# A gated three-branch token mixer: another first head, and weight sums made by the DMA

## The chip, the cores and the metric

The kernel runs on one core of one Trainium2 chip. The metric is the device time of one execution in microseconds (us); the median of the runs is what is compared.

## The reference

One layer over 512 tokens of width 2048, one batch, all in float32. The input is normed and projected once; the columns of this projection are the queries, keys, values and gate paths of three branches with four heads of 128 each, one forget logit per head, and three merge gates of width 2048.

```python
def hybrid_layer(x, norm_g, w_in, b_f, b_gate, qk_norm_g, rel_bias, w_up, w_out):
    hn = rmsnorm(x, norm_g)                       # x * rsqrt(mean(x*x) + 1e-6) * g
    proj = jnp.einsum('bsd,dc->bsc', hn, w_in)    # 2048 -> 3*4*512 + 4 + 3*2048 columns
    br = proj[..., :QKVG_COLS].reshape(b, s, N_BRANCH, 4, BRANCH_W)
    f_logit = proj[..., QKVG_COLS:QKVG_COLS + N_HEADS] + b_f
    gates = jax.nn.sigmoid(proj[..., QKVG_COLS + N_HEADS:] + b_gate).reshape(b, s, N_BRANCH, D_MODEL)
    ...                                           # A: forgetting attention, B: chunked attention with a
    ...                                           # relative bias, C: stick-breaking attention
    ys = jnp.stack([ya, yb, yc], axis=2) * jax.nn.silu(br[:, :, :, 3])
    up = jnp.einsum('bsnw,nwd->bsnd', ys, w_up)
    merged = jnp.sum(gates * up, axis=2)
    return x + jnp.einsum('bsd,de->bse', merged, w_out)
```

## The kernel before, in words

x lies transposed in 16 tiles of 128 rows of the model dimension by 512 tokens. TensorE's rounded float32 type is used throughout: every operand is split into a high part (ACT, L92) and a low part (DVE, L93), and `mm3` (L101 to L103) sums three products: high with high, low with high, high with low.

Most columns are computed two column tiles at a time. `pair_task` multiplies the 2x2 blocks of two tiles' weights (a11, a12 of the one, a21, a22 of the other, by halves of the model dimension) with the 2x2 blocks of x (halves of the model dimension by halves of the tokens) in seven products in place of eight, in Winograd's form of Strassen's method. One product is 8 k tiles of 3 matmuls of 256 columns. x's sides of products 1, 2, 3 and 5 are x's own parts (`x1`, `x2`) and a sum T1, those of 6, 7 and 4 are the sums T2, T3 and T4, made once by `combos`. The weights' sides of products 5, 7, 6 and 3 are sums of raw weight tiles: before, a pair loads its four raw tiles (512 KB each, `raw`, six buffers) through SP's queue, and DVE makes four sums of 128x1024 (L315 and those behind it). The order of the products is 1, 2, 6, 7, 4, 5, 3.

The program is a list of units (a product of a pair, or half a column by itself). The loop at the end runs through it: weights are split two units ahead of their matmuls (`prep_to`, `wh` and `wl`, three buffers each) and loaded seven units ahead (`load_to`). Its order for PE is kept as written for the first units (`OFF["man"]`); elsewhere a scheduler sets each engine's order.

`first_head` starts the run. Its units are the two halves of the forget logits (32 matmuls of 512 columns, x's high and low parts in turn) between those of Q and K, then V and G of the first head, each column by itself: 16 k tiles of 3 matmuls of 512 columns. `prep_x` splits x times its gain before the norm is known, and squares x; POOL and DVE share the running sum of squares. `norm_x` sums over the partitions with two full-precision matmuls (L247), and `rsqrt` makes rstd on ACT and DVE (L235 to L240), which is multiplied into Q, K, V, G as they leave PSUM. Then `combos` scales x itself (L255, DVE) and makes T2, T3 and T4 (L257 to L260, POOL), and `parts1`, `parts2` split the scaled x a second time into the same tiles. Two pairs of merge gate columns follow, then the other heads.

In all there are 54 pairs: 24 of gates, 22 of the heads (Q with K, V with G) and 8 of the output projection; the up projections are 32 units of 18 matmuls of 512 columns.

Of the kernel before, what the change touches and what calls it, by code (L numbers as in the profile page):

```python
# [38 lines left out]
def hybrid_kernel(  # L39
# [60 lines left out]
    def mm3(ps, lh, ll, rh, rl, start, stop):  # L100
        nc.tensor.matmul(ps, lh, rh, start=start, stop=False)  # L101
        nc.tensor.matmul(ps, lh, rl, start=False, stop=False)  # L102
        nc.tensor.matmul(ps, ll, rh, start=False, stop=stop)  # L103

    # ------------------------------------------------------------------ constants
# [18 lines left out]
    class Unit:  # L124
        """A stretch of the tensor engine's work with one stationary operand of up to 8 k tiles."""

        def __init__(self, shape, prep, mms, srcs=(), after=None):
            self.shape, self.prep, self.mms, self.srcs, self.after = shape, prep, mms, srcs, after
            self.hi = self.lo = None
# [4 lines left out]
    def load(u):  # L134
        u.raw = []
        for s, keep in u.srcs:
            t = raw_tile(u.shape)
            nc.sync.dma_start(t, s)
            u.raw.append(t)
            if keep is not None:  # L140
                keep.append(t)

    def prep(u):
        if u.shape is None:
            return
        u.hi = wp.tile([P] + u.shape, F32R, tag="wh", name=nm("wh"), bufs=LA + 1)
        u.lo = wp.tile([P] + u.shape, F32R, tag="wl", name=nm("wl"), bufs=LA + 1)
        u.prep(u)

    def prep_raw(u):  # L150
        split_to(u.hi, u.lo, u.raw[0])

    for kt in range(4):
        load_x(kt)
# [18 lines left out]
    # -1 where key k >= j: suffix sums inside a block  # L173
# [4 lines left out]
    # A, rows are queries: NEG where the key (free) is after the query  # L178
# [4 lines left out]
    # C, rows are keys: valid where the query (free) is after the key  # L183
# [7 lines left out]
    # column h has ones on the rows h, 32 + h, 64 + h, 96 + h  # L191
# [6 lines left out]
    # the query gains carry the softmax scale  # L198
# [16 lines left out]
    sqp = [att(), att()]  # L215

    def prep_x(kt):
        x = xraw[kt]
        h, lo = xs[kt]
        if kt % 2:  # L220
            nc.vector.tensor_scalar_mul(h, x, gn[:, kt:kt + 1])
        else:
            nc.scalar.activation(h, x, AF.Copy, scale=gn[:, kt:kt + 1])
        nc.vector.scalar_tensor_tensor(lo, x, gn[:, kt:kt + 1], f(h), op0=ALU.mult, op1=ALU.subtract)
        s = sqp[kt // 2 % 2] if kt % 2 and kt > 1 else t2("sq")
        nc.scalar.activation(s, x, AF.Square)
# [23 lines left out]

    def combos(k):
        """The rows of x at their norm, and what Strassen's form needs of them beside the parts."""
        a, b = xraw[k], xraw[k + UK]
        for x, kt in ((a, k), (b, k + UK)):
            nc.vector.scalar_tensor_tensor(x, x, gn[:, kt:kt + 1], rstd[0], op0=ALU.mult, op1=ALU.mult)  # L255
        t, u = t2("t23"), t2("t4")
        nc.gpsimd.tensor_sub(t[:, RH], b[:, RH], a[:, RH])  # L257
        nc.gpsimd.tensor_sub(a[:, RH], a[:, RH], a[:, LH])
        nc.gpsimd.tensor_sub(t[:, LH], b[:, RH], a[:, RH])
        nc.gpsimd.tensor_sub(u[:, LH], t[:, LH], b[:, LH])  # L260
        split_to(*t23[k], t)
        split_to(t4[k][:, LH], t4[k][:, RH], u[:, LH])
# [8 lines left out]
    # ------------------------------------------------------------------ projections  # L271
# [12 lines left out]
    def col_task(srcs, xs, evac):  # L284
        """A column tile as it stands; two units, one for each half of the rows."""
        ps = Lazy(acc)

        def mms(i):
            def go(u):
                for j in range(UK):  # L290
# [4 lines left out]
                     srcs=[(srcs[i], None)],  # L295
                     after=(lambda: evac(ps())) if i == 1 else None) for i in range(2)]

    def pair_task(src1, src2, ops, done, late=False, before_last=None):
        """Two column tiles by seven products in place of eight (Strassen, in Winograd's form).

        late: the products with T2, T3 and T4 come last."""
        kept = []
        st = {}
        w = {}
        order = (1, 2, 5, 3, 6, 7, 4) if late else (1, 2, 6, 7, 4, 5, 3)

        def prep_of(i):
            p = order[i]

            def go(u):  # L310
                if i == 0:
                    w[1], a21, w[4], w[2] = kept
                    split_to(u.hi, u.lo, w[1])
                    w[5] = raw_tile()
                    nc.vector.tensor_add(w[5], a21, w[4])  # L315
                    if late:
                        nc.vector.tensor_sub(a21, w[1], a21)
                        nc.vector.tensor_sub(w[1], w[5], w[1])
                    w[7], w[6], w[3] = a21, w[1], w[2]
                    return  # L320
                split_to(u.hi, u.lo, w[p])
                if i == 1:
                    if not late:
                        nc.vector.tensor_sub(w[7], w[1], w[7])
                        nc.vector.tensor_sub(w[6], w[5], w[1])
# [4 lines left out]
        def mms_of(i):  # L330
            def go(u):
                st["ps"] = ps = acc()[:, LH]
                for j in range(UK):
                    mm3(ps, u.hi[:, j, :], u.lo[:, j, :], *ops[order[i]](j), j == 0, j == UK - 1)
            return go

        def after_of(i):
            p = order[i]

            def go():  # L340
                ps = st["ps"]
# [8 lines left out]
                elif p == 6:  # L350
                    add(u[:, LH], u[:, LH], ps)
                    if late:
                        add(c1[:, RH], c1[:, RH], u[:, LH])
                elif p == 7:
                    add(u[:, RH], u[:, LH], ps)
                    if late:
                        add(c2[:, RH], c2[:, RH], u[:, RH])
# [4 lines left out]
                elif p == 5:  # L362
                    add(c2[:, RH], u[:, RH], ps)
                    add(u[:, LH], u[:, LH], ps)
                elif late:
                    add(c1[:, RH], c2[:, RH], ps)
                else:
                    add(c1[:, RH], u[:, LH], ps)
# [6 lines left out]
        src = {0: [(src1[0], kept), (src2[0], kept), (src2[1], kept), (src1[1], kept)]}  # L375
# [535 lines left out]
```

## Time and profile before

| what | us |
|---|---|
| median of 3 runs | 1400.05 (1399.22 to 1400.08) |
| span of the profiled execution | 1397.6 |
| PE busy | 1366.3 (98%) |
| DVE busy | 1191.8 (85%) |
| ACT busy | 729.7 (52%) |
| POOL busy | 53.7 (4%) |

The span is that of the instructions of one profiled execution; the median of the runs lies 2.45 us above it. PE is matmuls, DVE is VectorE, ACT is ScalarE, POOL is GpSimd, SP issues most of the DMAs. A row of a group of instructions reads: line, engine, operation, output<-input, shape and type, count, then busy time in all, mean time of one in ns, and the idle time before them with what ended it. A row of the chain of waits reads: start, duration, engine, what, line, count. Of a table of stages: the stretch and its length, busy time and count for PE, PEld (weight loads), DVE, ACT and POOL, then the granted clock of TensorE, the busy share of the DMA engines, and GB/s.

### The profile page before, as it was taken

The numbers are of one execution on the slowest core, as the hardware profiler recorded it, in microseconds if no ns is written. First come the engines' busy times: TensorE is split into PE (matmuls) and PEld (weight loads), VectorE is DVE, ScalarE is ACT, GpSimd is POOL, SyncE is SP. The second block draws the span as 40 slices with busy tenths as digits, with TensorE's granted clock in tenths as the row PEclk, the third lists the DMA queues.
The fourth block names the chain that finished last, engine by engine and source line by source line (L and its number), as shares of the span: only waits on it lengthen the run. The fifth ranks groups of instructions, "written<-read, shape, count | busy, mean of one in ns | idle before, by whom it ended". The sixth has DMA issues, their size and how long they took to land.

```text
span 1397.6 us, 25474 instructions
## 1 busy us (share of the span) xinstructions
PE 1366.3 (98%) x10452; PEld 1316.7 (94%) x10452; DVE 1191.8 (85%) x1671; ACT 729.7 (52%) x1042; POOL 53.7 (4%) x60
## 2 busy tenths in 40 slices
PE   6969999999999999999999999999999999999999
PEld 3759999999999999999999999999999988899999
DVE  8999898887978889888888888888888888898886
ACT  6345564544545555555556555545555755453332
POOL 4730000000000000000000000000000000000000
PEclk9989999999999999999999999999999999999999
DMA  7113334323344244342433333333233766535542
GB/s 272 46 46 106 122 102 126 121 91 114 106 129 126 95 114 128 113 129 95 117 122 115 121 94 119 113 114 121 91 115 103 273 197 203 169 109 176 164 151 76
DMA packets 63093, 176.39 MB, mean 126 GB/s; under 512 B 7400, under 2 KB 9320, under 8 KB 62976
## 3 DMA queue, kind: packets, MB, share of 16 engines
q1 hardware_dynamic: 59520, 170.49, 38.4%
q10 hardware_dynamic: 3456, 4.26, 0.8%
q8 instruction: 82, 1.34, 0.4%
q14 instruction: 35, 0.29, 0.1%
HBM read 155.04 MB, written 19.69 MB: 125 GB/s over the span
## 4 chain that ended last, share of the span: by engine, by line
PE 92%; DVE 5%; issue 1%; ACT 0%; POOL 0%; DMA 0%; SPq 0%; DVEq 0%; ACTq 0%; POOLq 0%
PE acc L101 27%; PE acc L103 27%; PE acc L102 27%; PE att L103 3%; PE att L101 3%; PE att L102 3%; DVE x L255 1%; DVE wl L93 1%; PE att L548 1%; PE att L517 1%; PE att L570 1%; DVE x1l L93 1%; PE att L571 1%; PE att L569 1%; DVE t23l L93 0%
## 5 line engine op out<-in xcount | busy, mean ns | idle before, releaser
L92 ACT ACTIVATE wh<-raw 128x1024 fp32r<-128x1024 f32 (+1 forms) x418 | 435.7, 1043 | 549.2 <-PE acc L102 488.2
L93 DVE TENSOR_TENSOR wl<-raw,wh 128x1024 fp32r<-128x1024 f32 (+1 forms) x418 | 503.9, 1206 | 96.7 <-ACT wh L92 95.9
L102 PE MATMUL acc<-x1l,wh 128*128 128x256 f32 (+1 forms) x768 | 222.3, 289 | 10.5 <-DVE x1l L93 10.5
L103 PE MATMUL acc<-x1h,wl 128*128 128x256 f32 (+1 forms) x768 | 222.0, 289 | 2.2 <-DVE wl L93 2.2
L101 PE MATMUL acc<-x1h,wh 128*128 128x256 f32 (+1 forms) x768 | 223.7, 291 | 0.0
L101 PE MATMUL acc<-x2h,wh 128*128 128x256 f32 (+1 forms) x768 | 223.6, 291 | 0.0
L102 PE MATMUL acc<-x2l,wh 128*128 128x256 f32 (+1 forms) x768 | 221.9, 289 | 0.9 <-DVE x2l L93 0.9
L103 PE MATMUL acc<-x2h,wl 128*128 128x256 f32 (+1 forms) x768 | 221.8, 289 | 0.0
L101 PE MATMUL acc<-t23h,wh 128*128 128x256 f32 x736 | 209.7, 285 | 0.0
L103 PE MATMUL acc<-t23h,wl 128*128 128x256 f32 x736 | 208.4, 284 | 0.0
L102 PE MATMUL acc<-t23l,wh 128*128 128x256 f32 x736 | 208.1, 283 | 0.0
L102 PEld LDWEIGHTS acc<-x1l,wh 128*128 128x128 f32 x768 | 147.8, 192 | 13.4 <-DVE x1l L93 11.2
L103 PEld LDWEIGHTS acc<-x1h,wl 128*128 128x128 f32 x768 | 147.8, 193 | 3.9 <-DVE wl L93 2.4
L102 PEld LDWEIGHTS acc<-x2l,wh 128*128 128x128 f32 x768 | 148.0, 193 | 2.4 <-DVE x2l L93 1.1
L101 PEld LDWEIGHTS acc<-x1h,wh 128*128 128x128 f32 x768 | 147.9, 193 | 1.8 <-issue 0.2
L101 PEld LDWEIGHTS acc<-x2h,wh 128*128 128x128 f32 x768 | 148.2, 193 | 1.3
L103 PEld LDWEIGHTS acc<-x2h,wl 128*128 128x128 f32 x768 | 148.0, 193 | 1.3
L101 PEld LDWEIGHTS acc<-t23h,wh 128*128 128x128 f32 x736 | 141.0, 192 | 0.5
L102 PEld LDWEIGHTS acc<-t23l,wh 128*128 128x128 f32 x736 | 141.0, 192 | 0.1
L103 PEld LDWEIGHTS acc<-t23h,wl 128*128 128x128 f32 x736 | 140.7, 191 | 0.3
L101 PE MATMUL acc<-t,wh 128*128 128x256 f32 x368 | 105.1, 286 | 0.0
L102 PE MATMUL acc<-t,wh 128*128 128x256 f32 x368 | 104.4, 284 | 0.0
(256 smaller groups left out, 2728.0 us busy)
## 6 DMA issues: line engine op xcount, KB each, us to landing
raw<-in_w_col SPq DMA_DIRECT2D x192, 512.0 KB, 3.6
raw<-in_w_out SPq DMA_DIRECT2D x32, 512.0 KB, 3.8
gl<-c SPq DMA_DIRECT2D x48, 256.0 KB, 2.0
raw<-in_w_up SPq DMA_DIRECT2D x32, 384.0 KB, 3.2
sg<-gl SPq DMA_DIRECT2D x48, 256.0 KB, 5.0
x<-in_xT SPq DMA_DIRECT2D x16, 256.0 KB, 5.4
xr<-in_xT SPq DMA_DIRECT2D x16, 256.0 KB, 4.4
yd<-y SPq DMA_DIRECT2D x11, 256.0 KB, 2.0
```

What stands on the lines that cost most here:

```text
L92: nc.scalar.activation(hi, src, AF.Copy)
L93: nc.vector.tensor_sub(lo, src, f(hi))
L101: nc.tensor.matmul(ps, lh, rh, start=start, stop=False)
L102: nc.tensor.matmul(ps, lh, rl, start=False, stop=False)
L103: nc.tensor.matmul(ps, ll, rh, start=False, stop=stop)
L255: nc.vector.scalar_tensor_tensor(x, x, gn[:, kt:kt + 1], rstd[0], op0=ALU.mult, op1=ALU.mult)
L517: nc.tensor.transpose(ps[:, blk(i)], st["p"][i][:, blk(j)], identf)
L548: nc.tensor.matmul(ps[:, i * P:], nu_r if i == j else nones_r, part, start=i == j and part is st["lk"][j][0], stop=False)
L569: nc.tensor.matmul(o, vh[:, blk(j)], st["h"][j], start=j == 0, stop=False)
L570: nc.tensor.matmul(o, vl[:, blk(j)], st["h"][j], start=False, stop=False)
L571: nc.tensor.matmul(o, vh[:, blk(j)], st["l"][j], start=False, stop=j == QB - 1)
```

## The change

*The first head.* x is scaled by its gain in place and is not split before the norm. Q and K (`first_pair`) are plain full-precision products of the raw weights with the scaled x, 2 x 16 matmuls of 512 columns; their weights are not split, and their raw halves are loaded between the x tiles, with quarters at first. ACT makes all squares, and DVE alone sums them. The sum over the partitions stands behind k tile 9 of Q and K. `split_x` then multiplies rstd into x and splits it, once; V and G and the forget logits use these parts and leave PSUM by a plain copy on ACT. `combos` works in place on x's halves, all on DVE, with T2 and T4 of the other sign, and `split_t1`, `split_t` split halves of 128x256. The order of the units is Q and K, V, G, V, G, the two halves of the forget logits, and then two gate pairs whose seven products alternate (1 of one, 1 of the other, 2, 2 and so on).

*The pairs.* With the signs changed every weight sum is an addition. Product 5's and product 7's weights are loaded as one raw tile by SP, onto which an accumulating DMA from POOL's queue (L324 of the changed kernel) adds the second; DVE makes the two that are left from them (6 is 5 plus 1, 3 is 6 plus 2, in place). The order is 5, 1, 2, 6, 7, 4, 3, and product 3 goes on in product 5's PSUM bank. In the two interleaved gate pairs and the first output pair ("late": 1, 2, 3, 5, 6, 7, 4) products 6 and 3 are made by accumulating DMAs too, two and three of them in a chain on one buffer. An ordinary pair moves 7 raw tiles in place of 4 (two for 5 and for 7, one each for 1, 2 and 4), a late one 14 (three for 6 and four for 3 besides).

```diff
-    def mm3(ps, lh, ll, rh, rl, start, stop):
+    def mm3(ps, lh, ll, rh, rl, start, stop, more=False):
...
     def load(u):
-        u.raw = []
-        for s, keep in u.srcs:
-            t = raw_tile(u.shape)
-            nc.sync.dma_start(t, s)
-            u.raw.append(t)
...
+        if u.load is not None:
+            u.load(u)
+        elif u.src is not None:
+            u.raw = raw_tile(u.shape)
+            nc.sync.dma_start(u.raw, u.src)
...
     def prep_x(kt):
         x = xraw[kt]
-        h, lo = xs[kt]
-        if kt % 2:
-            nc.vector.tensor_scalar_mul(h, x, gn[:, kt:kt + 1])
-        else:
-            nc.scalar.activation(h, x, AF.Copy, scale=gn[:, kt:kt + 1])
-        nc.vector.scalar_tensor_tensor(lo, x, gn[:, kt:kt + 1], f(h), op0=ALU.mult, op1=ALU.subtract)
-        s = sqp[kt // 2 % 2] if kt % 2 and kt > 1 else t2("sq")
+        s = t2("sq")
         nc.scalar.activation(s, x, AF.Square)
+        nc.scalar.activation(x, x, AF.Copy, scale=gn[:, kt:kt + 1])
         if kt < 2:
             ssq[kt] = s
         else:
-            (nc.gpsimd, nc.vector)[kt % 2].tensor_add(ssq[kt % 2], ssq[kt % 2], s)
+            nc.vector.tensor_add(ssq[kt % 2], ssq[kt % 2], s)
...
+    def split_x(kt):
+        nc.vector.tensor_mul(xraw[kt], xraw[kt], rstd[0])
+        split_to(*xs[kt], xraw[kt])
+
     def combos(k):
         a, b = xraw[k], xraw[k + UK]
...
+        nc.vector.tensor_sub(a[:, LH], a[:, LH], a[:, RH])
+        nc.vector.tensor_sub(a[:, RH], b[:, RH], a[:, RH])
+        nc.vector.tensor_add(b[:, RH], b[:, RH], a[:, LH])
+        nc.vector.tensor_sub(b[:, LH], b[:, RH], b[:, LH])
+
+    def split_t1(k):
+        (h, lo), a = x1[k], xraw[k]
+        split_to(h[:, RH], lo[:, RH], a[:, LH])
+
+    def split_t(k):
+        (h, lo), a, b = t23[k], xraw[k], xraw[k + UK]
+        split_to(h[:, LH], lo[:, LH], b[:, RH])
+        split_to(h[:, RH], lo[:, RH], a[:, RH])
+        split_to(t4[k][:, LH], t4[k][:, RH], b[:, LH])
...
-        order = (1, 2, 5, 3, 6, 7, 4) if late else (1, 2, 6, 7, 4, 5, 3)
+        order = (1, 2, 3, 5, 6, 7, 4) if late else (5, 1, 2, 6, 7, 4, 3)
+        (a11, a12), (a21, a22) = src1, src2
+        parts = {1: [a11], 2: [a12], 4: [a22], 5: [a21, a22], 7: [a11, a21]}
+        if late:
+            parts.update({6: [a21, a22, a11], 3: [a21, a22, a11, a12]})
+
+        def load_of(i):
+            def go(u):
+                p = order[i]
...
+                w[p] = raw_tile()
+                nc.sync.dma_start(w[p], parts[p][0])
+                for src in parts[p][1:]:
+                    nc.gpsimd.dma_start(w[p], src, accum_op=ALU.add)
+            return go
...
             def go(u):
-                if i == 0:
-                    w[1], a21, w[4], w[2] = kept
-                    split_to(u.hi, u.lo, w[1])
-                    w[5] = raw_tile()
-                    nc.vector.tensor_add(w[5], a21, w[4])
...
                 split_to(u.hi, u.lo, w[p])
-                if i == 1:
-                    if not late:
-                        nc.vector.tensor_sub(w[7], w[1], w[7])
-                        nc.vector.tensor_sub(w[6], w[5], w[1])
-                if i == (1 if late else 4):
-                    nc.vector.tensor_sub(w[3], w[3], w[6])
+                if not late and p == 1:
+                    w[6] = w[5]
+                    nc.vector.tensor_add(w[6], w[6], w[1])
+                elif not late and p == 6:
+                    w[3] = w[6]
+                    nc.vector.tensor_add(w[3], w[3], w[2])
...
+                more = p == 3 and not late
+                st[p] = ps = st[5] if more else acc()[:, LH]
...
+    def first_pair(st, n, h):
...
+            load_x(0)
+            w(Q, 0, 0, h4)
+            w(K, 0, 0, h4)
+            for kt in range(1, UK):
+                load_x(kt)
+            w(Q, 0, h4, UK)
+            w(K, 0, h4, UK)
+            for kt in range(UK, KT):
+                load_x(kt)
+            for r in cols:
+                w(r, 1, 0, UK)
+
+        def mms(u):
+            for kt in range(KT):
+                for r in cols:
+                    nc.tensor.matmul(ps[r](), raw[r, kt // UK][:, kt % UK, :], xraw[kt],
+                                     start=kt == 0, stop=kt == KT - 1)
+                if kt == OFF["ssq"]:
+                    with tc.high_priority():
+                        norm_x()
+
+        def after():
+            for kt in range(KT):
+                split_x(kt)
+            for r in cols:
+                st[r] = t2("c")
+                nc.vector.tensor_mul(st[r], ps[r](), rstd[0])
...
-        units.extend([fu[0], c[Q][0], c[K][0], fu[1], c[Q][1], c[K][1],
-                      c[V][0], c[G][0], c[V][1], c[G][1]])
+        units.extend([first_pair(st, n, h), c[V][0], c[G][0], c[V][1], c[G][1], fu[0], fu[1]])
+        pairs = []
+        for _ in range(2):
+            u0 = len(units)
+            gate_units(late=True)
+            pairs.append(units[u0:])
+            del units[u0:]
+        units.extend(u for two in zip(*pairs) for u in two)
...
-    prep_to(1)
-    load_to(2)
...
+    load_to(1)
+    for kt in range(KT):
+        prep_x(kt)
+    load_to(4)
...
-OFF = dict(cs=4, ct=12, nk=5, nq=4, s=12, t=16, v=1, av=8, a0=11, b0=18, c0=3, c1=2, man=17, last=3, l1=0, l2=0)
+OFF = dict(tf=2, cs=4, ct=12, nk=5, nq=4, s=12, t=16, v=1, av=8, ssq=9, fb=10, a0=8, b0=15, man=14, last=3)
```

The order of ACT's instructions before rstd. Before, ACT squares x (`sq`, `att`), scales some of it (`x2h`), splits weights (`wh`), and starts rstd (L235):

```order
L226 ACTIVATE att_194<-x_223 128x512
L92 ACTIVATE wh_372<-raw_310 128x1024
L226 ACTIVATE sq_301<-x_225 128x512
L226 ACTIVATE att_195<-x_227 128x512
L223 ACTIVATE x2h_185<-x_221,small_in 128x512
L92 ACTIVATE wh_403<-raw_312 128x1024
L223 ACTIVATE x2h_189<-x_225,small_in 128x512
L235 ACTIVATE rt_363<-att_359,epsc 128x512
```

In the changed kernel (`wh_303`, `wh_307` and `wh_412` are V's first half, G's first half and V's second half; rstd starts at L226):

```order
L92 ACTIVATE wh_307<-raw_297 128x1024
L216 ACTIVATE sq_279<-x_221 128x512
L217 ACTIVATE x_219<-x_219,small_in 128x512
L216 ACTIVATE sq_283<-x_223 128x512
L217 ACTIVATE x_221<-x_221,small_in 128x512
L217 ACTIVATE x_223<-x_223,small_in 128x512
L92 ACTIVATE wh_412<-raw_299 128x1024
L216 ACTIVATE sq_287<-x_225 128x512
L216 ACTIVATE sq_291<-x_227 128x512
L217 ACTIVATE x_225<-x_225,small_in 128x512
L217 ACTIVATE x_227<-x_227,small_in 128x512
L226 ACTIVATE rt_339<-att_335,epsc 128x512
```

The last two squares now stand behind three weight splits, all of V and G.

DVE's instructions up to the last low part of x's first half in the changed kernel, where L244 is the multiplication by rstd, L93 the low part and L670 the evacuation of Q:

```order
L244 TENSOR_TENSOR x_223<-x_223,rstd_338 128x512
L93 TENSOR_TENSOR x1l_144<-x_201,x1h_143 128x512
L93 TENSOR_TENSOR x1l_146<-x_203,x1h_145 128x512
L244 TENSOR_TENSOR x_225<-x_225,rstd_338 128x512
L93 TENSOR_TENSOR x1l_148<-x_205,x1h_147 128x512
L670 TENSOR_TENSOR c_408<-acc_313,rstd_338 128x512
L93 TENSOR_TENSOR x1l_150<-x_207,x1h_149 128x512
L244 TENSOR_TENSOR x_227<-x_227,rstd_338 128x512
L93 TENSOR_TENSOR x1l_152<-x_209,x1h_151 128x512
```

All 16 multiplications by rstd stand ahead of the last low part of x1; before, the 16 operations of L255 stood there one behind the other, with x's parts already in use by Q and K.

POOL's queue behind its constants, in the changed kernel (`raw_566` is product 3 of the first gate pair, `raw_607` that of the second; 635 and 719 are their products 5, 763 and 806 their products 6, 862 and 895 their products 7):

```order
L324 DMA raw_566<-in_w_col 128x1024 x3
L324 DMA raw_607<-in_w_col 128x1024 x2
L324 DMA raw_635<-in_w_col 128x1024
L324 DMA raw_607<-in_w_col 128x1024
L324 DMA raw_719<-in_w_col 128x1024
L324 DMA raw_763<-in_w_col 128x1024 x2
L324 DMA raw_806<-in_w_col 128x1024
L324 DMA raw_862<-in_w_col 128x1024
L324 DMA raw_806<-in_w_col 128x1024
```

Where the sums of squares and T2 to T4 stood on POOL, only these DMAs stand now, in this order in one queue.

More of the change, by code (lines that the diff above doesn't have):

```diff
@@ L150, in prep_raw @@
     def prep_raw(u):
-        split_to(u.hi, u.lo, u.raw[0])
-    for kt in range(4):
-        load_x(kt)
+        split_to(u.hi, u.lo, u.raw)
     epsc = cp.tile([P, 1], F32, name="epsc")
@@ L340, in go @@
             def go():
[L341 removed]
+                ps = st[p]
                 if i == 0:
@@ L361, in go @@
                     nc.scalar.activation(c2[:, RH], ps, AF.Copy)
[L362 to L368, printed above, removed]
+                    add(c1[:, RH], c1[:, RH], ps)
+                elif p == 3 and late:
+                    nc.scalar.activation(c1[:, RH], ps, AF.Copy)
+                elif p == 3:
+                    sub(c1[:, RH], ps, u[:, LH])
                 if i == 5 and before_last is not None:
@@ L373, in after_of @@
             return go
-        src = {0: [(src1[0], kept), (src2[0], kept), (src2[1], kept), (src1[1], kept)]}
-        return [Unit([UK, P], prep_of(i), mms_of(i), srcs=src.get(i, ()), after=after_of(i)) for i in range(7)]
+        return [Unit([UK, P], prep_of(i), mms_of(i), load=load_of(i), after=after_of(i)) for i in range(7)]
     side = {}
@@ L621, in hybrid_kernel, with load, w, kept @@
     cur = [0]
-    def scaled(st, r):
+    def first_pair(st, n, h):
+        cols = {r: col(n, r, h) for r in (Q, K)}
+        raw = {}
+        ps = {r: Lazy(acc) for r in cols}
+        def load(u):
+            def w(r, i, a, b):
+                if (r, i) not in raw:
+                    raw[r, i] = raw_tile()
+                nc.sync.dma_start(raw[r, i][:, a:b, :], cols[r][i][:, a:b, :])
+            h4 = UK // 2
+            load_x(0)
[23 more added lines that the diff above has]
+                nc.vector.tensor_mul(st[r], ps[r](), rstd[0])
+        return Unit(None, None, mms, load=load, after=after)
+    def kept(st, r):
         def evac(ps):
             st[r] = t2("c")
-            nc.vector.tensor_mul(st[r], ps, rstd[0])
+            nc.scalar.activation(st[r], ps, AF.Copy)
         return evac
@@ L631, in first_head, with sums, forget @@
         fu, fps = f_units()
[L632 to L641 removed]
+        c = {r: col_task(col(n, r, h), xs, kept(st, r)) for r in (V, G)}
+        units.extend([first_pair(st, n, h), c[V][0], c[G][0], c[V][1], c[G][1], fu[0], fu[1]])
[6 more added lines that the diff above has]
+        units.extend(u for two in zip(*pairs) for u in two)
+        def sums():
+            for k in range(UK):
+                combos(k)
         def parts1():
             for k in range(UK):
[L645 removed]
+                split_t1(k)
         def parts2():
             for k in range(UK):
[L649 removed]
+                split_t(k)
+        def forget():
             v = t2("f")[:2 * NH, :]
[L651 removed]
+            nc.scalar.activation(v, fps[:2 * NH, :], AF.Copy)
             nc.sync.dma_start(fd, v)
[L653 to L655 removed]
+            at(OFF["fb"], forget_bias)
+        at(OFF["tf"], sums)
+        at(5, parts1)
+        at(6, forget)
+        at(7, parts2)
         a, b = head_stages(n, h, st)
[L657 to L658 removed]
         for d, g in a:
```

85 lines of the change are left out of this document (21 added, 64 removed).

## The prediction

> **What bounds the kernel now.** I read the profile's page first: the engines' shares, the forty slices and the chain that ended last.
>
> ```profile
> span 1397.6 us, 25474 instructions
> PE 1366.3 (98%) x10452; PEld 1316.7 (94%) x10452; DVE 1191.8 (85%) x1671; ACT 729.7 (52%) x1042; POOL 53.7 (4%) x60
> ...
> PE   6969999999999999999999999999999999999999
> ...
> POOL 4730000000000000000000000000000000000000
> ...
> PE 92%; DVE 5%; issue 1%; ACT 0%; POOL 0%; DMA 0%; SPq 0%; DVEq 0%; ACTq 0%; POOLq 0%
> ```
>
> TensorE (PE) is the bound; 31 us of the span are not PE's, nearly all in the first three slices, where POOL has its only work. So I cut the run into stages (us, then busy time and instruction count by engine, granted clock, DMA share, GB/s).
>
> ```profile
> 0.00:95.00 95.00, 68.98 (x274) 49.50 (x274) 88.59 (x113) 46.29 (x74) 52.18 (x57) 0.93 0.33 118
> 95.00:1235.00 1140.00, 1139.98 (x8877) 1110.88 (x8878) 970.50 (x1383) 619.69 (x893) 1.51 (x3) 1.00 0.40 125
> 1235.00:1262.00 27.00, 24.98 (x202) 24.17 (x201) 25.77 (x40) 15.34 (x26) 0.00 (x0) 1.00 0.36 117
> 1262.00:1394.00 132.00, 132.00 (x1103) 132.00 (x1102) 106.52 (x137) 48.33 (x50) 0.00 (x0) 1.00 0.45 145
> ```
>
> From 95 us on PE has no idle time but 2.0 us between 1235 and 1262. In 0 to 95 us PE ran 274 instructions: 192 of the four columns Q, K, V, G, 32 of the forget logits, 4 of the sum of squares, which leaves 46 of the first pair of columns. The chain of waits names what holds PE there, VectorE (DVE):
>
> ```profile
> 6.02 0.60 ACT att L226
> 6.63 0.65 ACT x1h L223
> ...
> 33.82 0.70 DVE rw L239
> 34.61 0.70 DVE rstd L240
> ...
> 37.33 9.25 DVE x L255 x8
> ...
> 88.09 0.60 DVE x1l L93
> 88.69 0.61 DVE x2l L93
> ...
> 92.89 0.33 DVE t L93
> 93.23 1.14 DVE wl L93
> 94.36 0.61 DVE x2l L93
> ...
> 95.02 0.39 PE acc L102
> 95.41 0.12 PE acc L103
> 95.52 0.12 PE acc L101
> ```
>
> A matmul of 256 columns takes 0.12 us in a row of them. Had PE done nothing of the pairs before and run them without a gap, they would have begun at 95.0 - 46 x 0.12 = **89.5 us**. Everything behind is PE end to end, so the change is worth what it does to that moment, plus what it frees or adds at PE later.
>
> **The pace of single pieces**, from the order of time:
>
> ```profile
> 9.50 2.17 ACT L226 ACTIVATE sq<-x 128x512 f32<-128x512 f32 x4
> ...
> 20.55 0.63 PE L101 MATMUL acc<-x1h,wh 128*128 128x512 f32 x1
> 20.97 0.63 PE L102 MATMUL acc<-x1l,wh 128*128 128x512 f32 x1
> ...
> 25.64 0.40 PE L101 MATMUL acc<-x1h,wh 128*128 128x512 f32 x1
> 25.87 0.39 PE L102 MATMUL acc<-x1l,wh 128*128 128x512 f32 x1
> ...
> 28.37 2.00 PE L247 MATMUL att<-sq,tmpc 128*128 128x512 f32 x4
> 29.81 0.79 PE L101 MATMUL acc<-x1h,wh 128*128 128x512 f32 x1
> 30.44 0.40 PE L102 MATMUL acc<-x1l,wh 128*128 128x512 f32 x1
> ```
>
> A square is 0.54 us on ScalarE (ACT), a scaled copy 0.65. A rounded matmul of 512 columns is 0.43 us until 25.6 and 0.23 after: dense from 20.2, PE needed 5.1 us to reach full pace. L247 is the only full-precision product: two matmuls, four records, the last one from about 29.8 to 30.24, so 0.43 a record at full pace and 0.86 a matmul. Three rounded products are 0.68. From the last record's end to the end of rstd (34.61 + 0.70) it is 5.1 us.
>
> **The change, part by part.** *Q and K in full precision:* 32 matmuls x 0.86 = 27.5 us in place of 96 x 0.227 = 21.8, so 5.7 us more of PE, but no split of x or of their weights stands ahead. *When rstd is there:* up to the end of V's second weight split ACT holds 14 squares, 14 scaled copies and three weight splits:
>
> ```profile
> L92 ACT ACTIVATE wh<-raw 128x1024 fp32r<-128x1024 f32 x12 | 12.6, 1050 | 11.9 <-PE acc L102 11.7
> ...
> raw<-in_w_col SPq DMA_DIRECT2D x192, 512.0 KB, 3.6
> ...
> 0.00:20.00 20.00, 7.74 (x15) 1.14 (x15) 15.89 (x27) 12.40 (x19) 11.20 (x23) 1.00 0.93 350
> ```
>
> From 4.0 us that is 7.6 + 9.1 + 3.2 = 19.9. It waits 1.4 us for the fourth x tile, which now has two weight pieces ahead of it (I put it at 7.0, not 6.0), and 1.6 us for V's first weights: they end 6.8 MB, which at the 350 GB/s of the first 20 us is 19.5, and ACT is there at 17.9. So 26.9 us. DVE then takes the low part of that split (L93, 1.14) and the last two sums of squares, 0.60 each: 29.3. PE, from 8.3 us, does three slow matmuls (5.1 us) and 17 fast ones by 28.0, waits 1.3 us, does the sum (1.7), and ends Q and K at 29.3 + 1.7 + 12 x 0.86 = 41.3. rstd: 29.3 + 1.7 + 5.1 = 36.1.
> *x split once:* V's first product can't end before the last x1l, and DVE holds 24 operations of 128x512 and one evacuation up to it: 24 x 0.60 + 0.65 = 15.1, so 51.2. (0.60 is what it took at 88 us, beside an idle POOL.) The product ends 51.6; G, V, G follow, 3 x 24 x 0.227 = 16.3, and the 32 logits, 7.3: **75.2 us**. What hides the sums in place and the splits of T1 to T4 (8 x 8 halves, 64 x 0.33 = 21 us of DVE) is those 23.6 us and six products of x's own parts, 6 x 24 x 0.12 = 17.3 us. Without that cover each microsecond would be PE's.
> *The clock:* bounds are 0 and two coolings. A cooling costs 2.5 us (5.1 us at half pace, above). PE waits 3 us at 41.3 and is half busy up to 51.6, as before in a stage with clock 0.66:
>
> ```profile
> 80.00:100.00 20.00, 11.36 (x68) 10.87 (x69) 19.93 (x34) 9.76 (x17) 3.43 (x4) 0.66 0.21 57
> ```
>
> I take one, 2.5: the pairs begin at **77.7, 11.8 us earlier**. The Trainium skill (TensorE: Matmul & The Clock Gate, Part 1, HAM oscillation) has the clock fall only after gaps of more than about 3.4 us; by that rule the term is 0 and the whole 2.5 us less; no run here shows a gap of that length by itself.
> *Two interleaved gate pairs* (a and b, products 1 to 7): the split of 2b's weights stands in DVE behind 26 half operations. It should be done at about 85 us, where PE wants it at 86; I put 1.0 us, bounds 0 and 4.
> *Weight sums by DMA:* in an ordinary pair DVE loses two sums of 1.22 us (L325 and one of its kind), which PE never waited for after 95 us: worth nothing there.
>
> ```profile
> L325 DVE TENSOR_TENSOR raw<-raw,raw 128x1024 f32<-128x1024 f32 x36 | 43.9, 1219 | 0.3
> ```
>
> Only between 1235 and 1262, where DVE is busy 25.77 of 27 us, PE waits for it: four sums fewer (4.6 us) take away 1.5 of the 2.0, bounds 0 and 2. In return each ordinary pair moves 7 x 0.5 MB in place of 4. An accumulating transfer is not in the trace. Its landing, L, is bounded below by 3.6 (a plain 512 KB) and above by 7.2 (two of them, since it reads its target too); I take 5.4. An ordinary pair's tile is asked for seven products ahead: 7 x 24 x 0.12 = 20.2, less 3.6 for the plain part and 2.3 for the split, so L may be 14.3. The tight places are the three interleaved or late pairs, whose sums are chains. 3b: its buffer is free at 60.1, its plain part there at 63.7, three accumulations on it, wanted at 77.7 + 5 x 2.88 - 2.3 = 89.8: L up to 8.7. 6b: plain at 86.5, two on it, wanted at 101.3: 7.4. The first output pair's product 3: six units of 18 x 0.227 and two products, 24.5 + 5.8 less two splits and the plain part leaves 22 us for three: 7.4. So at 5.4 the cost is 0, and at the upper bound still 0. DMA share: 183 more transfers of 0.52 MB make 0.40 into about 0.62, or 0.83 if an accumulation counts twice.
> *POOL's sums go,* which stretched DVE beside them (rival below).
>
> Sum: -11.8 + 1.0 - 1.5 = **-12.3**, from 1397.6 a span of 1385.3. The median of the runs lies 2.45 above that span (1400.05): **1387.7 us**.
>
> **Rivals.**
> *Late sums (slower).* Mechanism: accumulations that take three plain landings, 10.8 us, because each is read, added and written by the engines that also bring the plain tiles. Then 3b comes at 96.1 against 89.8, 6.3 us; 6b 0.5; the output pair's product 3 by 36.0 against 25.7, 10.3: +17.1 and **1404.8**, slower. It decides from L = 10.1, where these waits eat the 12.3; from 14.3 every ordinary pair waits too, and at 16 us it costs 1.7 x 51 = 87 us more. For it: POOL issues in order, and a chain's next link waits for the one before. Against: DMA is free 60% of the time. 12%.
> *Nothing won at the start.* POOL beside DVE costs DVE time:
>
> ```profile
> L255 DVE SCALAR_TENSOR_TENSOR x<-x,small_in,rstd 128x512 f32<-128x512 f32 x16 | 14.6, 983 | 0.0
> ```
>
> 0.98 us, against 0.60 to 0.70 alone. From 45 us on POOL issues the accumulations of 3a. If writing those holds DVE as its sums did, the 24 operations take 24 x 0.38 = 9.1 us more: **1396.8**. A slow first 7 MB has the same effect: each us of V's weights is a us of the start. Against: one issue is no stream of sums. The Trainium skill (SBUF — State Buffer, SBUF: two separate sides) says that an operation with two SBUF inputs meets GpSimd only where GpSimd reads; by that rule this rival costs 0. 15%.
> *The change doesn't do what it says* (sums left on DVE, a split twice): the order shows both gone; no chance of its own.
>
> **How the numbers follow.** The forecast has 73%, with its own range 1381 to 1394: clock (-2.5 to +2.5), gates (-1 to +3), the late wait (-0.5 to +1.5), and some 2 us either way on the sum of squares. Late sums: 12%, a third of it near 1400. No gain at the start: 15%, of which 7 stay under 1397.2 and 2 pass 1402.9. The range **1381 to 1399** leaves out most of the late sums and a few of the best cases. What can't be told from no change here is 0.2%, 2.8 us: faster means below 1397.2. Faster: 0.73 + 0.07 = 0.80; same: 0.06 + 0.04 = 0.10; slower: 0.08 + 0.02 = 0.10.
>
> **What would show it.** Right: the sum's L238 matmuls at 28 to 31 us; rstd near 36; the last x1l near 51; the first matmul of the pairs at 75 to 79 and no idle PE behind it; L324 landings on POOL's queue under 7 us; the wait at 1240 to 1260 gone. Wrong: PE waiting for wl or wh of products 3 or 6 in the first 120 us, or of product 3 before the output stage (late sums); 128x512 operations near 1 us at 36 to 51 (POOL); half-pace matmuls past 60 us (more than one cooling); PE waits spread evenly over the ordinary pairs, which nothing in the sum has.

## The result, and the profile after

The changed kernel takes 1411.49 us (median of 4 runs, 1408.70 to 1414.40) against 1400.07 (median of 4 runs of the kernel before): 1.0082 times as long, 95% interval 1.0067 to 1.0096. The forecast was 1387.7. The profiled execution is the lowest of the four, 1408.70, with a span of 1406.7.

The page of the changed kernel (share of the span by engine, DMA queues, DMA issues):

```profile
span 1406.7 us, 25802 instructions
PE 1373.7 (98%) x10420; PEld 1313.6 (93%) x10420; DVE 1044.9 (74%) x1530; ACT 740.1 (53%) x1072; POOL 110.7 (8%) x144
...
q1 hardware_dynamic: 68448, 201.96, 44.3%
q0 software_dynamic: 17712, 64.50, 26.6%
...
raw<-in_w_col POOLq DMA_DIRECT2D x102, 512.0 KB, 6.7
```

VectorE lost 147 us of work, and PE is the bound as before. q0 is POOL's queue, 123 accumulations: 26.6% of all 16 DMA engines' time for 64.50 MB, where SP's queue took 44.3% for 201.96 MB. That is 3.04 us of all engines for an accumulation of 512 KB and 1.62 for a plain one.

The start is where it was forecast. The changed kernel's chain of waits, in order of time:

```profile
30.73 1.97 PE att L238 x4
...
36.07 0.70 DVE rstd L231
36.79 7.91 DVE x L244 x13
...
51.33 0.61 DVE x1l L93
51.98 0.50 PE acc L103
69.05 7.38 PE att L408 x32
```

The logits end at 76.3 and the pairs begin there. Stages of the changed kernel (stretch, then PE, PEld, DVE, ACT and POOL busy with counts, granted clock, DMA share, GB/s), and after them what PE waited for from there on (an entry has the sum, the number of waits and the longest; `wh` and `wl` are the high and low parts of a product's weights, `lkh` the high part of what the stick-breaking sums add up, `m2h` a high part of the output projection's input):

```profile
0.00:76.30 76.30, 61.82 (x197) 34.07 (x198) 55.22 (x112) 46.72 (x84) 8.08 (x24) 1.00 0.66 198
76.30:125.00 48.70, 42.33 (x323) 41.45 (x322) 32.16 (x77) 25.10 (x50) 8.44 (x10) 0.93 0.96 243
125.00:400.00 275.00, 269.11 (x2187) 267.37 (x2187) 201.57 (x283) 135.78 (x198) 20.94 (x25) 0.99 0.69 176
400.00:1230.00 830.00, 829.77 (x6345) 802.10 (x6344) 630.43 (x896) 462.54 (x659) 58.53 (x69) 1.00 0.71 191
1230.00:1252.00 22.00, 19.11 (x115) 17.22 (x114) 13.73 (x21) 10.26 (x14) 3.48 (x4) 0.92 1.03 249
```

```profile
PE att L557 <- ACT lkh L92: 5.9, 3, 2.0
PE acc L104 <- DVE wl L93: 5.2, 3, 4.3
PE acc L102 <- ACT m2h L92: 2.7, 1, 2.7
PE acc L102 <- ACT wh L92: 1.3, 1, 1.3
```

The waits alone are some 15 us; the matmuls behind several of them ran at half pace. So I took PE's order of time and summed, place by place, what stands between the starts of neighbouring matmuls beyond the pace of their size (0.12 us for 256 columns, 0.177 for 384, 0.227 for 512, 0.06 for 128). "Lost" means this sum, wait and slow matmuls together, from here on.

| place | before | after | difference | forecast |
|---|---|---|---|---|
| the pairs begin (gap-free) | 89.5 | 76.3 | -13.2 | -11.8 |
| interleaved gate pairs, 88 to 101 us | 0 | 7.2 | +7.2 | +1.0, both rows |
| the same, 111 to 117 us | 0 | 2.7 | +2.7 | |
| stick-breaking sums of three heads (187, 279, 370 us) | 1.7 | 11.2 | +9.5 | 0 |
| first output pair (1242 us) | 3.1 | 5.1 | +2.0 | -1.5 |

Together +8.2 of the spans' +9.1. The start gave what was promised, and three other places took it back. What held PE in the gate pairs stands in the same chain, from 77 to 113 us:

```profile
77.10 5.16 DMA fd<-f
...
82.67 7.92 DMA lf<-fd
...
91.19 1.23 DVE wl L93
...
101.33 10.26 DMA raw<-in_w_col
...
111.61 1.06 ACT wh L92
```

The forget logits (16 KB out to DRAM, 2 x 8 KB back) took 13 us, and DVE stood before the first operation on them with the low part of 3a's weights behind it; 6b's plain load was issued at 83.3 and landed at 91.7; its first accumulation took from 92.2 to 101.0, and its second from 101.3 to 111.6.

### The profile page after: what moved, and what is told of

Read it like the earlier page. It is cut to its first block, busy times and chain, and to the rows that moved or that the text cites. A ratio compares the mean times of both kernels' runs of the same rounds, so it can differ in the third digit from the quotient of the medians.

```text
span 1406.7 us, 25802 instructions
## 1 busy us (share of the span) xinstructions
PE 1373.7 (98%) x10420; PEld 1313.6 (93%) x10420; DVE 1044.9 (74%) x1530; ACT 740.1 (53%) x1072; POOL 110.7 (8%) x144
## 3 DMA queue, kind: packets, MB, share of 16 engines
q1 hardware_dynamic: 68448, 201.96, 44.3%
q0 software_dynamic: 17712, 64.50, 26.6%
## 4 chain that ended last, share of the span: by engine, by line
PE 90%; DMA 5%; DVE 2%; ACT 2%; issue 1%; SPq 0%; POOL 0%; POOLq 0%; DVEq 0%; ACTq 0%
PE acc L102 26%; PE acc L104 26%; PE acc L103 26%; PE att L103 2%; PE att L104 2%; PE att L102 2%; DMA raw<-in_w_out 2%; DMA raw<-in_w_col 2%; PE att L557 1%; DMA x<-in_xT 1%; DVE x L244 1%; PE att L526 1%; ACT wh L92 1%; DMA lf<-fd 1%; PE att L579 1%
## 5 line engine op out<-in xcount | busy, mean ns | idle before, releaser
L93 DVE TENSOR_TENSOR wl<-raw,wh 128x1024 fp32r<-128x1024 f32 (+1 forms) x414 | 497.9, 1203 | 147.9 <-ACT wh L92 142.9
L104 PE MATMUL acc<-x2h,wl 128*128 128x256 f32 (+1 forms) x752 | 216.0, 287 | 4.3 <-DVE wl L93 4.3
L103 PE MATMUL acc<-x1l,wh 128*128 128x256 f32 (+1 forms) x752 | 215.2, 286 | 2.8 <-DVE x1l L93 2.6
L102 PE MATMUL acc<-x2h,wh 128*128 128x256 f32 (+1 forms) x752 | 216.9, 288 | 0.0
L102 PE MATMUL acc<-x1h,wh 128*128 128x256 f32 (+1 forms) x752 | 216.8, 288 | 0.0
L103 PE MATMUL acc<-x2l,wh 128*128 128x256 f32 (+1 forms) x752 | 215.6, 287 | 0.0
L104 PE MATMUL acc<-x1h,wl 128*128 128x256 f32 (+1 forms) x752 | 214.4, 285 | 0.0
L324 POOL DMA_DIRECT2D raw<-in_w_col x102 | 88.2, 874 | 980.0 <-DMA raw<-in_w_col 519.5
L103 PEld LDWEIGHTS acc<-x1l,wh 128*128 128x128 f32 x752 | 143.4, 191 | 5.9 <-DVE x1l L93 5.2
L102 PE MATMUL acc<-t,wh 128*128 128x256 f32 x368 | 105.4, 286 | 0.0
```

The source lines that it names most:

```text
L93: nc.vector.tensor_sub(lo, src, f(hi))
L102: nc.tensor.matmul(ps, lh, rh, start=start, stop=False, skip_group_check=more)
L103: nc.tensor.matmul(ps, lh, rl, start=False, stop=False, skip_group_check=more)
L104: nc.tensor.matmul(ps, ll, rh, start=False, stop=stop, skip_group_check=more)
L324: nc.gpsimd.dma_start(w[p], src, accum_op=ALU.add)
```

## The experiments

**The forget logits emitted later.**

```diff
-OFF = dict(..., fb=10, ...)
+OFF = dict(..., fb=22, ...)
```

> One number of the changed kernel is altered: the work on the forget logits (their way through DRAM and the running sums on VectorE) is emitted 12 units later, behind the two interleaved gate pairs. Theory 1 (in the changed kernel VectorE stands 6.6 us in its order before the first operation on the logits that come back from DRAM, and the low part of 3a's weights is queued behind it): PE's wait of 4.3 us at 88 us and the half-pace matmuls behind it go, 7.2 us in all, from 1411.5 to 1404. Rival (3a's weights would be late anyway, by the splits ahead of them on VectorE or by their three accumulations): no change, 1411.5. Between them: PE is earlier at 6b, and its chain of accumulations takes back up to 5 us, 1406 to 1409.

1412.0 us (1410.5 to 1416.0), ratio 1.0090 (a ratio is against the kernel before, run beside it). This tells nothing of theory 1: the scheduler put that work back where it was. Row for row, every engine's order is that of the changed kernel; only tile numbers differ. It is a second look at the changed kernel, and there the interleaved pairs lost 9.0 and 4.8 us, the first output pair 7.1. Moving an emission is not moving an instruction.

**The scores a unit earlier.**

```diff
-OFF = dict(..., cs=4, ...)
+OFF = dict(..., cs=3, ...)
```

> One number of the changed kernel is altered: in the four stick-breaking heads the scores are emitted one unit (2.9 us) earlier, so that ACT and VectorE have 2.9 us more for the chain from the last scores to the sums (L557). Theory 1 (the scheduler put four weight splits and a weight sum of the new pairs into that chain, which took 15.3 us against 10.8 before, and PE waits 2.0 us and then runs at half pace for a while in three heads): the three waits go, 9.5 us, from 1411.5 to 1402. Rival (ACT and VectorE are themselves slower in these heads, or the chain only moves with PE): the waits stay, 1409 to 1411.5.

1403.23 us (1401.64 to 1405.77), ratio 1.0025: 8.3 less. The waits before L557 are gone; theory 1 for the heads holds. This run says something of the logits too. Its order of time on DVE, and its PE's waits from 76 us on:

```profile
84.18 0.23 DVE L423 SCALAR_TENSOR_TENSOR lf<-lf,small_in 128x16 f32<-128x16 f32 x1
```

```profile
PE acc L102 <- ACT wh L92: 8.4, 4, 4.3
PE acc L104 <- DVE wl L93: 2.7, 4, 0.8
```

Here the logits were back at 84, nothing stopped at 88, and the loss came at 101 to 120 us instead, 12.9 in place of 9.9. So the logits are a place where the loss can fall, and not its cause. In this run the first accumulation of 6a took 13.0 us; 6b's first, whose plain part was there at 89.2, stood behind 6a's second in POOL's queue until 97.1.

What the chain in the heads looks like. ACT in the changed kernel, from the last scores to the last high part that the sums need:

```profile
179.23 0.58 ACT L540 ACTIVATE z<-att 128x512 f32<-128x512 f32 x1
180.16 1.06 ACT L92 ACTIVATE wh<-raw 128x1024 fp32r<-128x1024 f32 x1 [0.35 <-PE acc L103]
181.13 0.51 ACT L543 ACTIVATE lk<-lk 128x384 f32<-128x384 f32 x1
181.60 1.06 ACT L92 ACTIVATE wh<-raw 128x1024 fp32r<-128x1024 f32 x1
182.57 0.62 ACT L543 ACTIVATE lk<-lk 128x512 f32<-128x512 f32 x1
183.09 1.03 ACT L544 ACTIVATE lk<-lk 128x384 f32<-128x384 f32 x2
184.48 1.06 ACT L92 ACTIVATE wh<-raw 128x1024 fp32r<-128x1024 f32 x1 [0.36 <-PE acc L103]
187.36 1.06 ACT L92 ACTIVATE wh<-raw 128x1024 fp32r<-128x1024 f32 x1 [1.82 <-PE acc L103]
188.33 1.02 ACT L92 ACTIVATE lkh<-lk 128x384 fp32r<-128x384 f32 x2
```

and in the kernel before, the same head:

```profile
183.57 0.58 ACT L531 ACTIVATE z<-att 128x512 f32<-128x512 f32 x1
185.18 1.06 ACT L92 ACTIVATE wh<-raw 128x1024 fp32r<-128x1024 f32 x1 [1.03 <-PE acc L102]
...
188.06 1.06 ACT L92 ACTIVATE wh<-raw 128x1024 fp32r<-128x1024 f32 x1
189.07 1.05 ACT L92 ACTIVATE lkh<-lk 128x384 fp32r<-128x384 f32 x2
...
190.94 1.06 ACT L92 ACTIVATE wh<-raw 128x1024 fp32r<-128x1024 f32 x1 [0.55 <-PE acc L102]
```

Four weight splits stand in the chain where two stood, and on DVE one of the two remaining weight sums (L337, 1.22 us) in front of L545. From z to the end of lkh it is 10.1 us against 6.6. PE wanted the sums at 187.4 and had them at 189.4.

The count of splits is not the whole of it. The last split stands directly in front of `lkh` and waited 1.82 us for PE: it could start at 187.36, when PE ended the product before the sums. Behind it comes `lkh`. So PE waits for one split (1.06) and `lkh` (0.94), the 2.0 us. In the kernel before, the split that waited for PE at this place (190.94) stands behind `lkh`. Without the split in front of `lkh`, PE would still have waited over 1 us in the changed kernel (an estimate: DVE's L546, which `lkh` needs and which runs behind the weight sum, ended at 187.7, and `lkh` takes 0.94).

**Single loads in place of the chains.**

```diff
-            parts.update({6: [a21, a22, a11], 3: [a21, a22, a11, a12]})
+            parts.update({6: [a11], 3: [a12]})
```

> Left out: the five accumulations behind the weights of products 6 and 3 in the two interleaved gate pairs and the first output pair, so that each of these is one plain load (15 transfers of 512 KB fewer; the sums in these three pairs are missing). Theory 1 (chains of accumulations land late at 6b and at the first output pair's product 3): the losses of 2.7 us at 111 us and of about 4 of 5.1 us at 1242 go, from 1411.5 to about 1405; the wait at 88 us stays, since it hangs on the forget logits. Rival (the transfers as a whole are late there, whichever they are): within 2 us of 1411.5.

1394.74 us (1394.30 to 1395.48), ratio 0.9963: 16.8 less, far more than theory 1's 6.5. Not only 6b and the output pair were healed, the stop at 88 went too: nothing is lost between 76 and 119 us, and 0.3 at 1238. The three heads' waits stay, as they should. So one cause stands behind both stops in the interleaved pairs: the chains. Theory 2 was formed on this.

**Both numbers altered.**

```diff
-OFF = dict(..., cs=4, ..., fb=10, ...)
+OFF = dict(..., cs=3, ..., fb=22, ...)
```

> Both numbers altered, that of the forget logits and that of the scores. If the two losses are separate causes, the gains add: 7.2 and 9.5, from 1411.5 to 1395. If one gives back what the other wins, 1400 or more.

1403.34 us (1401.19 to 1406.80), as with the scores alone, since the other edit moves nothing.

**Sums of the late pairs on VectorE** (with the scores a unit earlier):

```diff
-        order = (1, 2, 3, 5, 6, 7, 4) if late ...
+        order = (1, 2, 5, 3, 6, 7, 4) if late ...
-        if late:
-            parts.update({6: [a21, a22, a11], 3: [a21, a22, a11, a12]})
...
+                if late and p == 5:
+                    w[6], w[3] = w[1], w[2]
+                    nc.vector.tensor_add(w[6], w[6], w[5])
+                    nc.vector.tensor_add(w[3], w[3], w[6])
...
-                    add(c1[:, RH], c1[:, RH], ps)          # product 5, late
...
-                    nc.scalar.activation(c1[:, RH], ps, AF.Copy)   # product 3, late
+                    add(c1[:, RH], c2[:, RH], ps)
```

> In the two interleaved gate pairs and the first output pair the sums of products 6 and 3 are made by VectorE in place (6 is 1 plus 5, 3 is 2 plus 6), with the order 1, 2, 5, 3, 6, 7, 4, so that such a pair moves 7 raw tiles in place of 14; the scores are a unit earlier as in the run before. Theory 2 (the chains' accumulations fill the DMA engines from 60 to 112 us, 0.97 busy, and at 1226 to 1243; whichever load or logit comes last there is late, and where PE waits differs from run to run): the 12.9 us at 101 to 120 and some 4 of 6.2 us before the output stage go, from 1403.2 to 1386. Rival (VectorE has no room for four sums of 1.2 us at 75 to 100, where it is 100% busy up to 82): 3 to 5 us of it come back as waits for wl of products 3 and 6, 1389 to 1391.

1391.82 us (1390.16 to 1393.40), ratio 0.9937. The time misses both forecasts, and the trace tells the two places apart. In the interleaved pairs theory 2 holds to the end: 12.9 us became 0.8, with four sums on a DVE that was supposed to have no room. Before the output stage it does not: 6.3 us are lost as before, now with two DVE sums in the way there.

**The chains' accumulations as plain loads.**

```diff
-                    nc.gpsimd.dma_start(w[p], src, accum_op=ALU.add)
+                    if late and p in (3, 6):
+                        nc.gpsimd.dma_start(w[p], src)
+                    else:
+                        nc.gpsimd.dma_start(w[p], src, accum_op=ALU.add)
```

> The changed kernel, with the accumulations of products 6 and 3 in the late pairs turned into plain loads from the same queue onto the same tile, in the same chain (left out: the additions in them). Theory 2a (an accumulation's price is engine time: by the page's queue shares 64.5 MB took 26.6% of the engines' span there and 202 MB 44.3% here, 1.88 times as much a byte, 3.05 us of all engines in place of 1.62): 10 x 1.43 = 14 us of the 65 us of transfers at 45 to 112 go, most of the 9.9 us lost there and half of the 5.1 us at 1242, from 1411.5 to 1400 to 1403. Theory 2b (the price is the chain: each link is issued only when the one before has landed, behind others in POOL's order, and its bytes): nothing changes, 1409 to 1412.

1399.20 us (1396.83 to 1402.71): 12.3 less with the same links, the same order and the same bytes from memory. That is just under the 1400 to 1403 of theory 2a and far from 2b's 1409 to 1412, so 2a holds; 5.5 us are still lost at 104 to 113. POOL's queue took 25.7% of a span of 1397.4, against 24.1% of 1393.7 without the chains and 26.6% of 1406.7 with them: 359.1, 335.9 and 374.2 us of all engines. So a plain load of this queue costs (359.1 - 335.9) / 15 = 1.55 us and an accumulation (374.2 - 335.9) / 15 = 2.55.

**All ordinary sums on VectorE** (with the late pairs' sums on VectorE, the scores a unit earlier):

```diff
+                if not late:
+                    if p == 7:
+                        return
+                    for q, src in {5: [(7, a21), (4, a22)], 1: [(1, a11)], 2: [(2, a12)]}.get(p, ()):
+                        w[q] = raw_tile()
+                        nc.sync.dma_start(w[q], src)
+                    return
...
+                if not late and p == 5:
+                    w[5] = raw_tile()
+                    nc.vector.tensor_add(w[5], w[7], w[4])
...
                     nc.vector.tensor_add(w[6], w[6], w[1])
+                    nc.vector.tensor_add(w[7], w[7], w[1])
```

> As the run with the late pairs' sums on VectorE, and in the 51 ordinary pairs the sums of products 5 and 7 are made by VectorE too, from four raw tiles (two sums of 1.22 us more on VectorE and 3 transfers fewer in each pair; six accumulations are left in the kernel). If the accumulations of the ordinary pairs are worth nothing, as the prediction had it, the time is that of that run within 1.5 us. If VectorE's relief is worth something at the attention's chains, it is slower, by up to 10 us. If the traffic costs something in the ordinary pairs, it is faster by 1 to 3.

1388.99 us (1387.47 to 1389.37), ratio 0.9916 (0.9902 to 0.9929): the fastest kernel here, 11 us below the one before and 22 below the changed one. Its page:

```profile
span 1387.2 us, 25427 instructions
PE 1368.2 (99%) x10420; PEld 1310.0 (94%) x10420; DVE 1147.4 (83%) x1638; ACT 734.7 (53%) x1067; POOL 9.6 (1%) x27
```

2.8 us are won, though DVE does 96 us more, and the runs of the two kernels do not overlap. But neither trace shows that the accumulations' traffic had cost this in the ordinary pairs. 1.7 us are won before the output stage (4.6 lost in place of 6.3), where PE's two waits are the same 1.4 and 1.2 us in both and fewer matmuls run at half pace behind them; 1.2 are won at 1092 us, where PE waited for a high part of an up projection's input, ahead of which ACT loaded its tables three times (1.28 us each) and now does once; that points at the order again. Why the clock was lower for longer before the output stage, no run shows.

**The same with the scores at the changed kernel's place.**

```diff
-OFF = dict(..., cs=3, ...)
+OFF = dict(..., cs=4, ...)
```

> The run with all ordinary sums on VectorE, with the scores back at the changed kernel's place: six accumulations in all, and in three heads the same order on ACT and VectorE between the last scores and the sums as in the changed kernel (three and four weight splits and one weight sum in it). Theory 1 (that order alone makes the waits before the stick-breaking sums): the three waits return, 2.0 us and some half pace each, 8 to 10 us, from 1389.0 to 1397 to 1399. Rival (the accumulations' traffic slowed the operations or the loads behind them in these heads): 1389 to 1391.

1398.64 us (1397.13 to 1401.93): 9.7 more. With six accumulations in the whole kernel the three waits are back, to the row (PE's waits from 95 us on):

```profile
PE att L569 <- ACT lkh L92: 5.9, 3, 2.0
```

So the accumulations have no part in these waits; the order makes them. Which part of the change led the scheduler to it, the new order of the products or the other start, no run separates.

**Links of an eighth.**

```diff
-                    nc.gpsimd.dma_start(w[p], src, accum_op=ALU.add)
+                    part = slice(0, 1) if late and p in (3, 6) else slice(0, UK)
+                    nc.gpsimd.dma_start(w[p][:, part, :], src[:, part, :], accum_op=ALU.add)
```

> The changed kernel, with the accumulations of products 6 and 3 in the late pairs cut to one k tile of eight (64 KB in place of 512 KB; left out: the rest of these sums). The chains keep their links, each issued when the one before has landed, in the same order on POOL. Theory 2a (engine time, of which 7/8 of the accumulations' share goes): as without chains, 1394 to 1396. Theory 2b (the number of links, each with its issue and its landing): the loss of 2 to 5 us at 6b and of some 4 us before the output stage stay, 1399 to 1405.

1394.01 us (1392.97 to 1395.01), as without chains (1394.74): links, issues and landings by themselves cost nothing that can be measured, what they carry costs all. Of the 16.8 us between the changed kernel and the one without chains, turning the accumulations into plain loads wins 12.3, and the plain loads' own transfers are left with 4.5. POOL's queue, where a late link holds up those behind it, passes a delay on, but does not make one. The stretch of 80 to 112 us in the changed kernel, with plain links, with small links and without chains (columns as in the stages above, the DMA share last but one):

```profile
80.00:112.00 32.00, 27.11 (x199) 26.42 (x197) 16.29 (x43) 11.12 (x24) 6.13 (x8) 0.89 1.00 238
```

```profile
80.00:112.00 32.00, 28.75 (x224) 27.91 (x223) 21.17 (x51) 15.97 (x32) 4.55 (x7) 0.96 0.91 251
```

```profile
80.00:112.00 32.00, 32.00 (x266) 31.86 (x265) 24.69 (x58) 18.54 (x37) 5.21 (x6) 1.00 0.78 192
```

```profile
80.00:112.00 32.00, 32.00 (x266) 31.86 (x265) 27.52 (x63) 20.64 (x41) 2.57 (x3) 1.00 0.81 224
```

At a share of 1.00 PE stood 4.9 us and ran at 0.89 of its clock; at 0.81 it never stopped. The rate of bytes is not what was short: 238 GB/s at the share of 1.00, 251 with plain links at 0.91.

**The first output pair's chains back, alone** (on the fastest kernel, with the order 1, 2, 5, 3, 6, 7, 4):

```diff
-            units.extend(pair_task(out_col(e), out_col(e + 1), mops, both, late=True))
+            units.extend(pair_task(out_col(e), out_col(e + 1), mops, both, late=True, chain=True))
+        if chain:
+            parts.update({6: [a21, a22, a11], 3: [a21, a22, a11, a12]})
...
-                if late and p == 5:
+                if late and p == 5 and not chain:
```

> The run with all ordinary sums on VectorE (1389.0), but in the first output pair products 6 and 3 come by accumulating DMAs again, in the order 1, 2, 5, 3, 6, 7, 4. With the ordinary traffic gone a link should land in about 7 us, and product 3 is wanted 25 us after its buffer is free, so that the sums are there in time and VectorE has 2.4 us less to do where PE waited 1.4 and 1.2 us for it: 3 to 4 us less, 1385 to 1386. Rival (the links take 7.5 us or more beside the up projections' loads): 1388 to 1391.

1392.10 us (1391.56 to 1393.13), 3.1 more: the forecast was wrong, and the time lies even above the rival's 1388 to 1391. Two links of its chain of waits, and what PE waited for:

```profile
1212.90 7.80 DMA raw<-in_w_out
...
1220.98 7.80 DMA raw<-in_w_out
```

```profile
PE acc L102 <- ACT wh L92: 3.6, 1, 3.6
```

A link takes 7.8 us there; 7.5 was the point from which the rival decides.

## Why the prediction was wrong

**The start** was right: PE's sum at 30.7 (28 to 31), rstd done at 36.8 (36.1), the last x1l at 51.9 (51.2), the pairs at 76.3 (77.7). The 1.4 us of difference are less than the cooling I had put at 2.5. The clock was granted in full from 0 to 76 us, so that term was 0; without it the forecast was 75.2. By the Trainium skill's rule (TensorE: Matmul & The Clock Gate, Part 1, HAM oscillation) the wait of 2.1 us there was too short; but in the fastest kernel's profile the clock fell to 0.83 behind the same wait (42 to 52 us), and the pairs still began at 76.4, since DVE's last x1l held them. The term had no place in the sum. POOL's issuing did not slow DVE: its first accumulation was issued from 47.75 to 48.76, and DVE's operations beside it took 0.60 us each, as did the 13 multiplications by rstd before (7.91 us, 0.61 each), so that rival fell.

**Accumulating DMAs, the tight places.** The mechanism that I gave 12% came: the chains' sums were late. Its price, 17.1 us against the 16.8 by which the kernel without chains is faster, was right by accident. The step that failed is "So at 5.4 the cost is 0, and at the upper bound still 0": it took L as a property of a single transfer, and the DMA share as a mean over the run (0.62 to 0.83). A link landed in 6.7 us in the median, inside my bounds, and in up to 11.9 between 40 and 125 us. What was to be counted is the stage. From 45 to 112 us POOL issued 14 accumulations and SP 10 plain loads, at 3.04 and 1.62 us of all engines 58.8 of the 67 us, and the DMA queues of that stretch (packets, MB, share of 16 engines) say the same:

```profile
q0 software_dynamic: 1973, 7.23, 59.8%
q1 hardware_dynamic: 1954, 5.81, 24.6%
```

The share was 0.48 from 40 to 60 us and 1.00 from 80 to 112. From 80 us on the engines were full, and what came then was late: the plain part of 6b (forecast for 86.5, there at 91.7), its links (8.8 and 10.3 us, where 7.4 was the most that they could take), and 32 KB of logits on which DVE happened to stand. 3b, the other tight place, was in time: its last link landed at 85.4. Which of these PE meets differs from run to run; a loss there is in each (9.9, 12.9, 13.8 and 14.4 us in four profiles of kernels with these chains). My rival had 6.8 us for 3b and 6b and 10.3 for the output pair; measured are 9.9 and, against the run without chains, 4.8. Two side figures of the prediction were off, with no part in this: by the rival's own terms the waits reach 12.3 us at an L of 9.8, not 10.1, and of the 183 further transfers only 123 accumulate, so that counting those twice gives a share of 0.76, not 0.83.

**Interleaved gate pairs.** I put 1.0 us on 2b's splits, with bounds of 0 and 4. Without the chains nothing was lost there, and with four sums more on DVE 0.8. The bounds were right, and DVE had room; that 0.8 is near 1.0 is luck, since it belongs to another order of DVE's work.

**Ordinary pairs, "worth nothing there".** The step counted what DVE is relieved of and looked for waits on DVE in the trace of before. It did not look at what the new order puts between an attention head's scores and its sums, though the rows of the order were there to be read: four weight splits for two on ACT, the last of them in front of `lkh` and waiting for PE, and a weight sum on DVE. The kernel before had 0.7 us to spare at that place (sums ready at 190.1, wanted at 190.9), which no term of mine held. It cost 9.5 us, and comes back whole (9.7) in a kernel where DVE makes all the ordinary sums.

**The first output pair.** I expected 1.5 us from four sums fewer on DVE. With the chains, product 3's last link held its high part, and m2's high part stood behind that on ACT: 2.0 more than before in the profiled run.

**The range** left out exactly what happened: two costs, one of 14.7 us (9.9 and 4.8), a rival at 12%, and one of 9.5, unseen. With the sums on DVE and the scores a unit earlier, the start's gain comes through: 1389.0. That this is 1.3 from the 1387.7 of the forecast does not bear the forecast out: the sums are made elsewhere than it assumed, and the output stage still loses 4.6 us.

## What to carry to other kernels

A transfer that replaces an engine's work is priced in the stage where it runs, as the time of all DMA engines against the stage's length, not by its latency or by the share over the run. When a change alters the order of units, read the static order of every engine between two ends of a dependent chain with little slack, not only the busy time, above all for an instruction ahead of the chain that itself waits for the engine at the chain's end. And after an edit that is meant to move work, look whether the order moved before reading anything from the time.

## What the runs showed of the hardware that I had not expected

An accumulating transfer of 512 KB takes 2.55 to 3.04 us of all 16 engines, where a plain one takes 1.55 to 1.62: 1.6 to 1.9 times as much.

PE can fall to half pace after a wait of only 2.0 us. Four stretches behind waits of the changed kernel: three behind equal waits of 1.96 us before the stick-breaking sums, and one behind 4.3 us (stretch, PE busy and count, granted clock, DMA share, GB/s):

```profile
189.40:193.80 4.40, 4.40 (x24) 0.63 0.86 220
281.00:285.00 4.00, 4.00 (x24) 0.71 0.78 240
372.40:376.40 4.00, 3.83 (x31) 1.00 0.79 213
...
92.40:97.40 5.00, 4.94 (x23) 0.50 0.99 207
```

The first two lost some 1.4 us more than the third, and behind the wait of 2.1 us at 43 us the clock was full in this execution and 0.83 in the fastest kernel's. The Trainium skill's rule of more than about 3.4 us (TensorE: Matmul & The Clock Gate, Part 1, HAM oscillation) does not separate these cases; what does, no run here shows.
